# The low part of each weight tile formed by ScalarE's negated copy and an adding DMA, in place of VectorE's subtraction

## Chip, cores and metric

One core of one Trainium2 chip runs the kernel. The metric is the device time of one launch in microseconds (us). TensorE (PE) multiplies matrices, VectorE (DVE), ScalarE (ACT) and GpSimd (POOL) work on tiles in on-chip memory, and transfers are issued from the queues of SyncE (SP), ScalarE and GpSimd and carried by 16 DMA engines.

## What is computed

One layer of a decoder trunk for 512 prompt tokens and 8 sample tokens, model width 1024, everything in float32:

```python
x = x + W_out( sig(g_A) * (A(rmsnorm(x)) @ W_pA) + sig(g_B) * (B(rmsnorm(x)) @ W_pB) )
x = x + W_down( relu(rmsnorm(x) @ W_up)^2 )
# A: chunked gMLP spatial gating; B: 4 heads of chunkwise retention with a 256x512 state per head
# outputs: rmsnorm(x) of prompt and samples, new states of prompt and of the 8 samples, the gMLP's v rows
```

## The kernel before

Activations lie feature-major, 128 features by two halves of 260 tokens. The weights are the stationary operand. A float32 product is made of three passes over parts of lower precision: a weight tile is split into `wh`, the tile rounded to float32r, and `wl`, what the rounding left off, and the activations likewise (`xh`, `xl`). `prod` (L184) then issues wh*xh, wh*xl and wl*xh for both token halves: six matmuls for each 128-row slice of the weights.

All weights stream through one list of blocks, 88 of 1 MB, in the order of use (`build_stream`, L125). SP loads a block into one of three `raw` buffers (`load_to`, L147). A block is cut into four halves of 128x4x128 numbers (512 numbers on each partition, in four runs of 128). The generator `split` (L160) turns one half into a pair of tiles: L166 writes `wh` on ScalarE, L168 writes `wl` on VectorE, and the pair is entered in `wt`. There are five buffers each of `wh` and `wl` (`LA + 1`). `take` (L176) hands half i to the matmuls and before that starts the split of half i + 4. So the `wh` of half i + 4 takes the buffer that half i - 1 has just given up. A half is 24 matmuls. The first four halves are split apart from this, in `first_split` (L283); the other 348 go through `split`.

Work beside the stream is written as generators; `micro` (L76) moves each of them on by a step between matmuls, and a bare `yield` is one such step. This sets the order of the instructions on each engine by hand; every engine and queue works its instructions off in that order. The program's stages by the profile's time: the gMLP branch (to about 235 us), four retention heads (about 235 to 685), the joining of the branches and `w_out` (to about 765), the FFN (to about 1122), and the last norm.

Three places outside the stream matter. In the heads `samples` (L793) loads 64 slices of state on the SP queue (`sp_load`, L787), scales each on ScalarE (L821), updates it on VectorE (L823), stores it from the GpSimd queue (L824) and sums from it (L829), with four `sp` buffers. The GpSimd queue also carries the other stores to HBM and short power operations of the norms (L313, L707, L1043). A `raw` buffer is loaded anew (L158) when the last reader of the block that it held is done.

Of the kernel before, what the change touches and what calls it, by code (L numbers as in the profile page):

```python
# [11 lines left out]
AF = mybir.ActivationFunctionType  # L12
ALU = mybir.AluOpType
# [20 lines left out]
def f32(ap):  # L34
    return ap.bitcast(F32)
# [5 lines left out]

@with_exitstack
def trunk_kernel(ctx: ExitStack, tc: tile.TileContext, t: dict, o: dict):
    """Activations lie feature-major, [128 features, 2 halves, 256 prompt + 4 sample tokens]; the weights are the
    stationary operand. A float32 product runs as three float32r passes over exact parts (hi rounded to
    float32r, lo = x - hi): hi*hi + hi*lo + lo*hi. Work beside the weight stream is written as generators
    that advance between the matrix products."""
    nc = tc.nc
    V, S, PE, G = nc.vector, nc.scalar, nc.tensor, nc.gpsimd
    gam = [1.0 - 2.0 ** (-5.0 - h) for h in range(NH)]  # L50
# [10 lines left out]

    w_in = t["w_in"][0]

# [1 line left out]
    tasks, done = [], set()  # L65

    def advance(T):
# [30 lines left out]
            n += 1  # L98
            assert n < 2000, [k for k in keys if k not in done]

# [1 line left out]
    blocks, halves = [], []  # L102

    def add_block(src, uses):
# [55 lines left out]
    def split(i):  # L160
        b, k0, c0, _ = halves[i]
        load_to(b + (2 if i and halves[i - 1][0] == b else 1))
        src = raw_t[b][:, k0:k0 + 4, c0:c0 + 128]
        wh = st["wpool"].tile([P, 4, 128], R, tag="wh", bufs=st["wbufs"], name="wh")
        wl = st["wpool"].tile([P, 4, 128], R, tag="wl", bufs=st["wbufs"], name="wl")
        S.activation(out=wh, in_=src, func=AF.Copy)  # L166
        yield
        V.tensor_tensor(out=wl, in0=src, in1=f32(wh), op=ALU.subtract)  # L168
        wt[i] = (wh, wl)

    def split_to(n):
# [45 lines left out]
        return r[:, :512].rearrange("p (a b) -> p a b", a=4)  # L217

    def hilo(oh, ol, src):
        """Two steps: the rounded part, then the rest."""  # L220
        S.activation(out=oh, in_=src, func=AF.Copy)
        yield
        V.tensor_tensor(out=ol, in0=src, in1=f32(oh), op=ALU.subtract)
# [7 lines left out]
    def halves_of(pt):  # L231
        return pt.rearrange("p (h a) b -> p h (a b)", h=2)

# [1 line left out]
    gm = ExitStack()  # L235
    xp = ExitStack()
    xpool = xp.enter_context(tc.tile_pool(name="xpool", bufs=1, side="right"))
# [33 lines left out]
    for i in range(N_WARM):  # L271
        PE.matmul(ps_w[:, i % 2, :256], lhsT=warm[:, :P], rhs=warm, start=True, stop=True)

# [1 line left out]
    xh = xpool.tile([P, 8, 2, HC], R, name="xh")  # L275
    xl = xpool.tile([P, 8, 2, HC], R, name="xl")
    X = (xh, xl)
# [35 lines left out]
        G.tensor_tensor(out=dst, in0=dst, in1=neghalf[:n, :dst.shape[-1]], op=ALU.pow)  # L313

    def bcast_rows(rs, out, lag):
        """rs: [128, 5] per token (4 chunks, then the samples); out: [128, 2, 260], along the partitions."""
        dg = base.tile([P, 2 * HC], F32, tag="m4", bufs=2, name="dg")
        for c in range(4):
            V.tensor_scalar(out=dg[:, 128 * c:128 * (c + 1)], in0=ident, scalar1=rs[:, c:c + 1], scalar2=None,
                            op0=ALU.mult)  # L320
        V.tensor_scalar(out=dg[:NS, 512:520], in0=ident[:NS, :NS], scalar1=rs[:NS, 4:5], scalar2=None, op0=ALU.mult)
        yield lag
        pa = x_tile()
        pb = x_tile()
        PE.matmul(pa.rearrange("p a b -> p (a b)"), lhsT=ones, rhs=dg[:, :512], start=True, stop=True)
        PE.matmul(pb[:, 0, :8], lhsT=ones[:NS, :], rhs=dg[:NS, 512:520], start=True, stop=True)
        yield 2
        V.tensor_copy(out=out[:, :, 0:256], in_=halves_of(pa))
        V.tensor_copy(out=out[:, :, 256:HC], in_=hs8(pb[:, 0, :8]))
# [3 lines left out]
    rst = base.tile([P, 5], F32, name="rst")  # L333

    def token_rsqrt(pool, sq, key, lag):
        """rb = rsqrt(mean over the features + eps) from the sums of squares left on the partitions."""
        rs = rst
        sqs = pool.tile([P, 8], F32, name="sqs")
        V.memset(rs, 1.0)
        V.tensor_copy(out=hs8(sqs), in_=sq[:, :, 256:HC])  # L340
        yield lag[0]
        pt = x_tile()
        for c in range(4):
            hh, off = ccols(c)
            PE.matmul(pt[:, 0, c:c + 1], lhsT=sq[:, hh, off:off + 128], rhs=ones[:, 0:1], start=True, stop=True)
        PE.matmul(pt[:NS, 0, 4:5], lhsT=sqs, rhs=ones[:, 0:1], start=True, stop=True)
        yield
        V.tensor_copy(out=rs[:, 0:4], in_=pt[:, 0, 0:4])
        V.tensor_copy(out=rs[:NS, 4:5], in_=pt[:NS, 0, 4:5])
        rsqrt_mean(rs, rs, 1.0 / DM)  # L350
        yield lag[1]
        yield from bcast_rows(rs, rb, lag[2])
        done.add(key)
# [18 lines left out]
        V.tensor_tensor(out=z, in0=ps[:, :, :HC], in1=rb, op=ALU.mult)  # L372
        return z

# [1 line left out]
    smpv = gpool.tile([P, 8, 8], F32, name="smpv")  # L376
    lng = gpool.tile([P, DM], F32, name="lng")
    lnb = gpool.tile([P, DM], F32, name="lnb")
# [192 lines left out]
        micro()  # L571
    gm.close()

# [1 line left out]
    late = ctx.enter_context(tc.tile_pool(name="late", bufs=1))  # L575
    acc = late.tile([P, 8, 2, HC], F32, tag="acc", name="pbacc")
    hs = ExitStack()
# [31 lines left out]
    def make_head(h):  # L609
        H = Head()  # L610
        g = gam[h]
# [66 lines left out]
            done.add(("s", h))  # L678

        def v_task(e, ps):  # L680
            """v stays unscaled; its tokens' factors go into k and the scores."""
            z = tmp()
            S.copy(out=z, in_=ps[:, :, :HC])
            V.tensor_tensor(out=hs8(H.smp[:, 4 + e, :]), in0=z[:, :, 256:HC], in1=rb[:, :, 256:HC], op=ALU.mult)
            done.add(("vs", h, e))
            yield 2
            yield has(("s", h))
            if e == 0:
                H.vh = hp.tile([P, 4, DV], R, tag="vkh", name="vh")
                H.vl = hp.tile([P, 4, DV], R, tag="vkl", name="vl")  # L690
            pt = x_tile()
            for c in range(4):
                hh, off = ccols(c)
                PE.transpose(pt[:, c, :], z[:, hh, off:off + 128], ident)  # L694
            yield
            es = slice(128 * e, 128 * (e + 1))
            yield from hilo(H.vh[:, :, es], H.vl[:, :, es], pt)
            done.add(("vt", h, e))
# [14 lines left out]
            done.add(("o", h, c))  # L713

        def steps():
            """o of each chunk, token-major, and the state's update."""
            yield has(("kt", h), ("s", h), *[("vt", h, e) for e in range(4)])
            yield 2
            st_ps = ps_s.tile([P, 2, DV], F32, tag="st", name="st_ps")
# [70 lines left out]
                nc.sync.dma_start(out=H.sp[i], in_=sview[:, :, i, :])  # L790

        def samples():
            """The state's step of the samples: partitions hold (sample, 16 blocks of 16 rows of the state)."""  # L793
            yield has(*([("rs", h - 1)] if h else []), *[("vs", h, e) for e in range(4)])
            yield 3
            for j in range(2):
# [114 lines left out]
    until(*[("gb", m) for m in range(8)])  # L911
    xp.close()

# [1 line left out]
    f0s = ExitStack()  # L915
    f0 = f0s.enter_context(tc.tile_pool(name="f0", bufs=1, side="right"))
    h2 = (f0.tile([P, 8, 2, HC], R, name="hh_t"), f0.tile([P, 8, 2, HC], R, name="hl_t"))
# [61 lines left out]

    spawn(ffn_norm(), now=False)  # L980

# [1 line left out]
    F = {}  # L983

    def up_task(fh, f, ps):
# [19 lines left out]
        F["rs"] = pool.tile([P, 2, 3], F32, name="rs3")  # L1005

    def fin_task(m, ps, hhs):
        """x2 = x1 + the FFN's output; the sums of its squares, the last d-tile's apart."""
        a, b = hhs[0], hhs[-1] + 1
        x = x1[:, m, a:b]  # L1010
        V.tensor_tensor(out=x, in0=x, in1=ps[:, a:b, :HC], op=ALU.add)
        yield 1 if m == 7 else 1
        z = F["sq"][:, a:b] if m == 0 else F["z"][:, a:b] if m == 7 else tmp()[:, a:b]
        S.activation(out=z, in_=x, func=AF.Square)
        if 0 < m < 7:
            yield
            V.tensor_tensor(out=F["sq"][:, a:b], in0=F["sq"][:, a:b], in1=z, op=ALU.add)
        done.update(("fin", m, hh) for hh in hhs)
# [1 line left out]
    cols = (slice(0, 128), slice(128, 256), slice(HC - 128, HC))  # L1020

    def fin_norm(hh):
        """Token sums over the features, the samples' in the last rows of the third column."""
        yield has(*[("fin", m, hh) for m in range(7)])
        yield 17
        if hh:
# [77 lines left out]


def constants():
    """Tables that depend on shapes and positions alone."""
    a = np.arange(DK // 2, dtype=np.float32) * (np.float32(1) / np.float32(DK // 2 - 1))
    a[-1] = 1.0
    inv = np.float32(1) / (10000.0 ** a.astype(np.float64)).astype(np.float32)  # L1110
    pos = np.full((2, HC), PAST, np.float32)
    pos[0, :256] = np.arange(256)
    pos[1, :256] = np.arange(256, 512)
    ang = (inv[:, None, None] * pos[None]).astype(np.float32).astype(np.float64)
    j = np.arange(P, dtype=np.float64)
    tab = np.zeros((P, 544), np.float64)
    for h in range(NH):
        g = 1.0 - 2.0 ** (-5.0 - h)
        tab[:, 128 * h:128 * (h + 1)] = np.where(j[None, :] >= j[:, None], g ** -j[:, None], 0.0) / 16.0
        for c in range(4):  # L1120
            tab[:, 512 + 4 * h + c] = g ** -(128.0 * c + j) / 16.0
        tab[:, 528 + h] = g ** j
        tab[:, 532 + h] = g ** (2 * j) / DV
    for s in range(NS):
        tab[16 * s:16 * (s + 1), 536 + s] = 1.0
    return {"c_ident": np.eye(P, dtype=np.float32), "c_tab": tab.astype(np.float32),
            "c_cos": np.cos(ang).astype(np.float32), "c_sin": np.sin(ang).astype(np.float32)}
# [44 lines left out]
```

## Time and profile before

| | |
|---|---|
| time, median of two runs | 1148.82 us (1146.76 to 1150.87) |
| span of the profiled execution | 1145.0 us |
| granted TensorE clock over it | 0.995 of full speed |
| TensorE busy | 1125.9 us, 98% |
| VectorE / ScalarE / GpSimd busy | 670.1 / 476.3 / 89.2 us |
| moved by DMA | 148.05 MB |

The span runs from the first to the last instruction of one profiled execution; the runs' times contain a little more around it. Busy time of an engine leaves out the issuing of DMAs on SP and ScalarE, while GpSimd's own issues are counted. A DMA share is the mean share of time in which the 16 DMA engines worked on packets. An idle engine costs nothing by itself; what counts is whether the matmuls have to wait.

### The profile page before, as it was taken

Reading aid. Unit: us, or ns where it says so; the run is one execution under the profiler, and the core shown is the slowest. Engines: PE = TensorE matmul, PEld = TensorE weight load, DVE = VectorE, ACT = ScalarE, POOL = GpSimd, SP = SyncE. Lnnn points to the kernel's source line nnn. Section 1 sums busy time; section 2 is a strip of 40 time slices with the busy share of each in tenths; the row PEclk is TensorE's granted clock in tenths of the full one; section 3 lists DMA queues with packets and bytes.
Section 4 is the critical chain, followed back from the end, with each engine's and each line's share of the span. In section 5 each row is a group of like instructions: output and inputs, shape, how many; then the busy total and the mean of one; then the engine's idle time right before and its main releaser. Section 6 shows DMA issues by size and latency. Waiting matters only on the chain.

```text
span 1145.0 us, 21897 instructions
## 1 busy us (share of the span) xinstructions
PE 1125.9 (98%) x9134; PEld 1107.8 (97%) x9134; DVE 670.1 (59%) x1178; ACT 476.3 (42%) x844; POOL 89.2 (8%) x148
## 2 busy tenths in 40 slices
PE   8999999999999989999999999999999999999996
PEld 8999999999999989999999999999999999999996
DVE  6567833554984488477846878555553234554333
ACT  6465522246555545554555543432332222333220
POOL 0000000002110210120102120000000000000000
PEclk9999999999999999999999999999999999999998
DMA  8423233224673475356634795623232323232302
GB/s 290 130 82 103 76 112 129 94 74 141 183 205 126 117 218 177 100 146 194 172 120 117 206 316 160 194 77 109 74 110 76 111 74 109 77 106 80 100 12 75
DMA packets 116628, 148.05 MB, mean 129 GB/s; under 512 B 9576, under 2 KB 93736, under 8 KB 116528
## 3 DMA queue, kind: packets, MB, share of 16 engines
q1 hardware_dynamic: 101712, 118.73, 32.8%
q0 software_dynamic: 12336, 24.72, 7.8%
q10 hardware_dynamic: 2480, 3.19, 0.8%
q8 instruction: 72, 1.18, 0.5%
q14 instruction: 28, 0.23, 0.1%
HBM read 121.16 MB, written 25.43 MB: 128 GB/s over the span
## 4 chain that ended last, share of the span: by engine, by line
PE 83%; issue 8%; DMA 3%; DVE 2%; POOL 2%; ACT 1%; SPq 0%; ACTq 0%; POOLq 0%; DVEq 0%
PE mm L189 75%; PE xps L730 2%; PE st_ps L736 2%; DMA sp<-in_state_ret 2%; POOL out_new_s L824 1%; PE xps L694 1%; DMA xT<-in_xT 1%; PE ps_v L189 1%; DMA out_new_s<-sp 0%; DVE sp L823 0%; DVE wl L168 0%; PE xps L799 0%; ACT sp L821 0%; DVE so L829 0%; DVE x L1058 0%
## 5 line engine op out<-in xcount | busy, mean ns | idle before, releaser
L166 ACT ACTIVATE wh<-raw 128x512 fp32r<-128x512 f32 x348 | 218.9, 632 | 462.0 <-PE mm L189 442.9
L168 DVE TENSOR_TENSOR wl<-raw,wh 128x512 fp32r<-128x512 f32 x348 | 238.6, 688 | 201.3 <-ACT wh L166 199.7
L189 PE MATMUL mm<-xh,wh 128*128 128x260 f32 x1264 | 261.0, 288 | 2.2 <-ACT wh L287 0.8
L189 PE MATMUL mm<-xl,wh 128*128 128x260 f32 x1264 | 254.7, 283 | 0.3 <-DVE xl L294 0.3
L189 PE MATMUL mm<-xh,wl 128*128 128x260 f32 x1264 | 254.8, 283 | 0.0
L189 PEld LDWEIGHTS mm<-xh,wh 128*128 128x128 f32 x1264 | 196.2, 189 | 5.7 <-ACT wh L287 1.1
L189 PEld LDWEIGHTS mm<-xl,wh 128*128 128x128 f32 x1264 | 195.1, 189 | 0.8 <-DVE xl L294 0.8
L189 PEld LDWEIGHTS mm<-xh,wl 128*128 128x128 f32 x1264 | 195.4, 189 | 0.0
L189 PE MATMUL mm<-ah,wh 128*128 128x260 f32 x640 | 134.3, 283 | 0.0
L189 PE MATMUL mm<-ah,wl 128*128 128x260 f32 x640 | 134.1, 283 | 0.0
L189 PE MATMUL mm<-al,wh 128*128 128x260 f32 x640 | 134.0, 283 | 0.0
L189 PE MATMUL mm<-gh,wl 128*128 128x260 f32 x512 | 103.2, 283 | 0.0
L189 PE MATMUL mm<-gh,wh 128*128 128x260 f32 x512 | 103.2, 283 | 0.0
L189 PE MATMUL mm<-gl,wh 128*128 128x260 f32 x512 | 103.0, 283 | 0.0
L189 PEld LDWEIGHTS mm<-ah,wh 128*128 128x128 f32 x640 | 100.9, 188 | 0.0
L189 PEld LDWEIGHTS mm<-ah,wl 128*128 128x128 f32 x640 | 100.9, 188 | 0.0
L189 PEld LDWEIGHTS mm<-al,wh 128*128 128x128 f32 x640 | 100.6, 188 | 0.0
L372 DVE TENSOR_TENSOR tmp<-mm,rb 128x520 f32<-128x520 f32 x69 | 48.2, 698 | 72.0 <-PE mm L189 71.9
L189 PEld LDWEIGHTS mm<-gh,wh 128*128 128x128 f32 x512 | 78.9, 188 | 0.0
L189 PEld LDWEIGHTS mm<-gh,wl 128*128 128x128 f32 x512 | 79.0, 188 | 0.0
L189 PEld LDWEIGHTS mm<-gl,wh 128*128 128x128 f32 x512 | 78.7, 188 | 0.0
L824 POOL DMA_DIRECT2D out_new_s<-sp x64 | 39.2, 612 | 218.0 <-DVE sp L823 205.4
(280 smaller groups left out, 1467.1 us busy)
## 6 DMA issues: line engine op xcount, KB each, us to landing
raw<-in_w_in SPq DMA_DIRECT2D x39, 1024.0 KB
sp<-in_state_ret SPq DMA_DIRECT2D x64, 256.0 KB
out_new_s<-sp POOLq DMA_DIRECT2D x64, 256.0 KB, 5.0
raw<-in_w_up SPq DMA_DIRECT2D x16, 1024.0 KB
raw<-in_w_down SPq DMA_DIRECT2D x16, 1024.0 KB
raw<-in_w_proj_ret SPq DMA_DIRECT2D x8, 1024.0 KB
raw<-in_w_proj_gm SPq DMA_DIRECT2D x4, 1024.0 KB
raw<-in_w_out SPq DMA_DIRECT2D x4, 1024.0 KB
```

The source lines that it names most:

```text
L166: S.activation(out=wh, in_=src, func=AF.Copy)
L168: V.tensor_tensor(out=wl, in0=src, in1=f32(wh), op=ALU.subtract)
L189: PE.matmul(ps[:, hh, :HC], lhsT=w[:, j, :], rhs=x[:, k, hh, :], start=(first and q == 0), stop=(last and q == 2))
L372: V.tensor_tensor(out=z, in0=ps[:, :, :HC], in1=rb, op=ALU.mult)
L694: PE.transpose(pt[:, c, :], z[:, hh, off:off + 128], ident)
L730: PE.matmul(po, lhsT=a, rhs=b, start=(n == 0), stop=(n == len(mms) - 1))
L736: PE.matmul(st_ps[:, d, :], lhsT=a[:, c, ks], rhs=b[:, c, :], start=(c == 0 and n == 0), stop=(c == 3 and n == 2), skip_group_check=True)
L824: G.dma_start(out=oview[:, :, i, :], in_=sp)
```

## The change

After the rounding to `wh`, ScalarE writes `wl` too: a copy of `wh` times -1. One step of the generators later a DMA is issued from the GpSimd queue that adds the raw half onto it, so that `wl` = -wh + raw. VectorE's subtraction goes. `take` may hand the pair out at the same point of the program as before, since the DMA stands where the subtraction stood. `first_split` is as it was.

```diff
         S.activation(out=wh, in_=src, func=AF.Copy)
-        yield
-        V.tensor_tensor(out=wl, in0=src, in1=f32(wh), op=ALU.subtract)
+        S.activation(out=wl, in_=f32(wh), func=AF.Copy, scale=-1.0)
+        yield
+        G.dma_start(out=wl, in_=src, accum_op=ALU.add)
         wt[i] = (wh, wl)
```

Besides, comments and docstrings are blanked out, which leaves the instructions alone; behind L168 all lines move down by one.

## Rows read from the trace of the kernel before

**Rows 1.** The page: span, engines' busy time and share, the chain by engine.
```profile
span 1145.0 us, 21897 instructions
...
PE 1125.9 (98%) x9134; PEld 1107.8 (97%) x9134; DVE 670.1 (59%) x1178; ACT 476.3 (42%) x844; POOL 89.2 (8%) x148
...
PE 83%; issue 8%; DMA 3%; DVE 2%; POOL 2%; ACT 1%; SPq 0%; ACTq 0%; POOLq 0%; DVEq 0%
```
**Rows 2.** Timeline of ScalarE in the FFN: start, duration, instruction, idle before.
```profile
880.91 0.63 ACT L166 ACTIVATE wh<-raw 128x512 fp32r<-128x512 f32 x1 [2.23 <-PE mm L189]
883.81 0.63 ACT L166 ACTIVATE wh<-raw 128x512 fp32r<-128x512 f32 x1 [2.27 <-PE mm L189]
```
**Rows 3.** Stretches: length, busy of PE, PEld, DVE, ACT, POOL, clock, DMA share, GB/s.
```profile
2.00:28.00 26.00, 24.24 (x189) 22.67 (x188) 17.95 (x33) 17.79 (x33) 0.00 (x0) 1.00 0.94 318
...
235.00:685.00 450.00, 443.31 (x3486) 430.32 (x3485) 307.16 (x562) 236.12 (x443) 71.88 (x117) 1.00 0.55 162
```
**Rows 4.** Stretches, VectorE's `wl` alone: length, busy (count), clock, DMA share, GB/s.
```profile
28.00:140.00 112.00, 22.59 (x33) 1.00 0.30 95
140.00:235.00 95.00, 22.36 (x33) 1.00 0.35 118
235.00:300.00 65.00, 11.39 (x17) 1.00 0.38 111
300.00:340.00 40.00, 8.28 (x12) 1.00 0.74 207
340.00:390.00 50.00, 8.28 (x12) 1.00 0.38 120
390.00:430.00 40.00, 7.48 (x11) 1.00 0.70 199
430.00:560.00 130.00, 26.14 (x38) 0.99 0.53 154
560.00:685.00 125.00, 24.73 (x36) 1.00 0.62 187
685.00:765.00 80.00, 19.16 (x28) 1.00 0.52 163
765.00:1122.00 357.00, 83.66 (x122) 1.00 0.26 83
```
**Rows 5.** The chain that ended last, in order of time: start, length, what.
```profile
38.33 0.69 DVE wl L168
...
395.97 5.29 DMA sp<-in_state_ret
...
409.22 8.32 DMA sp<-in_state_ret
```
**Rows 6.** Waits: who waited for whom, us in total, times, longest.
```profile
POOL out_new_s L824 <- DVE sp L823: 205.4, 58, 8.1
...
SPq L158 <- DVE wl L168: 694.0, 65, 18.3
SPq L790 <- DMA out_new_s<-sp: 193.7, 47, 11.0
```
**Rows 7.** The page's costliest groups: the two halves of the split.
```profile
L166 ACT ACTIVATE wh<-raw 128x512 fp32r<-128x512 f32 x348 | 218.9, 632 | 462.0 <-PE mm L189 442.9
L168 DVE TENSOR_TENSOR wl<-raw,wh 128x512 fp32r<-128x512 f32 x348 | 238.6, 688 | 201.3 <-ACT wh L166 199.7
```
**Rows 8.** The state's stores at L824: durations (ns) on GpSimd, and to landing.
```profile
L824 POOL DMA_DIRECT2D out_new_s<-sp x64: 596/598/872, 279.8 to 673.9; - x64
...
DMA to landing us min/median/max: 3.9/5.0/8.5
```
**Rows 9.** DMA queues from 815 to 950 us, SP's: packets, MB, share of 16 engines.
```profile
q1 hardware_dynamic: 12346, 12.46, 28.7%
```
**Rows 10.** DMA queues from 235 to 685 us, GpSimd's own.
```profile
q0 software_dynamic: 11264, 21.23, 17.8%
```

## Prediction

> **What bounds the kernel now.** I read the page first: TensorE is busy for 98% of a span of 1145.0 us, and the chain that ended last runs through it for 83% [rows 1]. VectorE (59%) and ScalarE (42%) are far from full. All that TensorE leaves idle is 1145.0 - 1125.9 = 19.1 us, 1.7%, start and end included, so relief for another engine can't be worth more than that; in the heads it is 450 - 443.31 = 6.7 us [rows 3].
>
> Next the timeline, to see how much room a weight half has. In the FFN ScalarE begins a `wh` every 2.9 us, idle before each for 2.2 us until TensorE gives a buffer up [rows 2]. A half of 24 matmuls thus takes 2.9 us, and this is the period of the stream. By the code the `wh` that begins when half i - 1 ends belongs to half i + 4, so four halves lie between, 4 x 2.9 = 11.6 us. Today's split takes 0.63 + 0.69 us of that: about 10 us of slack.
>
> Then the stretches, for the DMA engines. Their share is 0.55 over the heads [rows 3], but 0.26 in the FFN and 0.62 to 0.74 in three parts of the heads [rows 4]. There the state's loads lie on the chain, 5.3 and 8.3 us long [rows 5], and SP waits 193.7 us for state stores to land before it can load again [rows 6]. So in the FFN only TensorE is short; in the heads TensorE and DMA are both near their limits.
>
> **The change, part by part.**
>
> *Removed:* 348 subtractions of 688 ns, 239 us of VectorE [rows 7]. They are hidden behind matmuls except where VectorE runs late; the gain lies between nothing and the 6.7 us of gaps in the heads. I take nothing, since the same places also wait for state loads.
>
> *Added on ScalarE:* 348 copies of the shape of L166, so 348 x 0.632 = 220 us [rows 7]; ScalarE goes from 476 to 696 us, 61%. In the FFN the second copy fits into the 2.2 us idle before each `wh` [rows 2]; over the heads 236 us becomes 236 + 126 x 0.63 = 315 us of 450 [rows 3, 4]. I cost it at nothing; were the cover gone it would be 0.63 us for each half that TensorE waits for.
>
> *Added latency:* `wl` is ready when the DMA has landed. The nearest rows are stores of the same 256 KB from the same queue: 3.9 us to landing at least, 5.0 median, 8.5 at most [rows 8]. With two copies (1.3 us) that makes 6.3, typically, and 9.8 at worst, under 11.6. In the steady stages nothing is lost. At the start the chain runs through a `wl` at 38.33 us [rows 5], where 0.69 us is replaced by about 5: +5 us, rounded up for the first halves.
>
> *Added on the GpSimd queue:* 348 issues between stores and power operations. A DMA of 128 runs takes 0.60 us there [rows 8]; an adding one has 512 runs of 512 bytes. From below it takes 0.6 us, if runs cost nothing; from above 4 x 0.6 x 3/2 = 3.6 us, if time goes with runs and two reads and a write count for three instead of two. I take about 1.2, nearer to the lower end, because an issue's time has a part that doesn't depend on runs; then 348 x 1.2 = 418 us lies beside the matmuls. An add waits on its queue for ScalarE, which waits for TensorE, up to 2.3 us [rows 2]; queued behind it are the state's stores, and for them SP's next state load. The other way round an add stands behind a store that waits up to 8.1 us for VectorE [rows 6]. VectorE's subtraction stood behind the same instruction, so only the DMA's own latency is new.
>
> *Moved on SP's queue:* a `raw` buffer is free when the last add has landed, some 5 us later than now. SP's wait at L158 (694 us in 65 [rows 6]) grows by that. A block is next used nine halves, 26 us, later, so the weights come in time; state loads queued behind it are late by up to 5 us.
>
> *Added on the DMA engines,* which decides. An add has 128 x 4 = 512 runs, 32 for each of the 16 engines. In the FFN the weight loads' packets, 1 KB each, take 0.287 x 16 x 135 us / 12346 = 50 ns [rows 9]. A run is 512 bytes read from raw, 512 read from `wl`, and 512 written. If the two reads go one after the other, it costs a 1 KB packet: 32 x 50 ns = 1.6 us an add. From below, half a packet, as a plain copy of 512 bytes might cost: 0.8 us. From above, one packet of the GpSimd queue in the heads, 0.178 x 16 x 450 / 11264 = 114 ns [rows 10]: 3.6 us. I take 1.6, since the bytes read are those of the first row, and that row too goes into on-chip memory, while the last one is mostly stores to HBM.
>
> *The sum.* Work of the DMA engines in a stretch is share x length, plus 1.61 us for each add, one for each subtraction of today [rows 4]. Back-to-back loads at the start reach a share of 0.94 [rows 3], so a stretch can't be shorter than work / 0.94. This gives:
> 300 to 340: (29.6 + 19.3) / 0.94 = 52.0, +12.0;
> 390 to 430: (28.0 + 17.7) / 0.94 = 48.6, +8.6;
> 430 to 560: (68.9 + 61.2) / 0.94 = 138.4, +8.4;
> 560 to 685: (77.5 + 58.0) / 0.94 = 144.1, +19.1;
> 685 to 765: (41.6 + 45.1) / 0.94 = 92.2, +12.2.
> In the FFN (92.8 + 196.4) / 0.94 = 308 stays under 357 us, +0; the other four stretches stay under too (28 to 140 us, the fullest: (33.6 + 53.1) / 0.94 = 92 of 112). Together +60, with the start +65: 1145 + 65 = 1210 us of span. The median of the runs is 3.8 us above the profiled span, so 1214 us.
>
> **The rivals.** *Hidden (the other side: not slower).* The DMA engines take an add in 0.8 us, as a copy. Then only 300 to 340 is over its length, (29.6 + 9.6) / 0.94 = 41.7, +1.7, and with the start's 5 the time is 1156 us; with the 6.7 us of gaps won back, 1149. It decides below about 1.1 us an add, where the loss falls under 2%. For it: the slack of 10 us covers the latency. Against it: an add has to read its target as well.
> The Trainium skill, "DMA: Bandwidth & Descriptors", section on the anatomy of one DMA on the GpSimd path, fits 2.0 us plus bytes / 436 GB/s to one DMA; by that an estimate for 256 KB is 2.6 us, of which 0.6 us is movement, and this rival would hold at about 1150 us. The trace shows 3.9 to 8.5 us to landing for stores of that size [rows 8], longer than the rule.
> Another page, "Collectives: The Full Stack", section "The bandwidth ceiling", speaks against this rival: an add in a DMA needs two source reads on one ring and so moves at half a copy's rate. No row of the kernel before shows an add.
>
> *The add is dearer than the stream's period.* If DMA engines or GpSimd need more than a half's 2.9 us, less the weight loads, every stage waits, the FFN too; it decides from (357 x 0.94 - 92.8) / 122 = 2.0 us an add on the DMA engines. At the middle between my value and the upper bound, 2.6 us, the same sum gives +82 in the FFN, +165 in the heads, +42 in the stage behind them and +48 before them: about 1490 us. If it is GpSimd at 3.6 us, 348 x 3.6 + 89 = 1342 us. For it: 512 short runs in place of 128 on a queue that a program feeds, and nothing in the trace that adds. Against it: the issue rows are flat at 0.60 us.
>
> *Faster.* All 6.7 us in the heads and some of the rest come back: 1138 us at best by the traced gaps, under 1%. More than 2% is beyond the 19.1 us that there are.
>
> **How the numbers follow.** DMA engines full in the heads and behind them, 1172 to 1290 us: 0.40, the likeliest, 1214 us. Hidden: 0.31, of which 0.01 faster. Dearer than the period: 0.29. The range leaves out the upper part of the dear case (0.12) and a small part of the hidden one: 1142 to 1490 us. About 2%, 23 us, is what a measurement of this kernel tells from no change. Slower by more: 0.40 + 0.29 = 0.69, less 0.01 for the lower edge of the likeliest case, 0.68; within 2%: 0.31; faster: 0.01.
>
> **What would show it.** VectorE's L168 is gone (about 430 us busy), ScalarE is near 696 us. The GpSimd group for `wl` has 348 issues: a mean of 0.9 to 1.5 us is right, over 2.9 wrong. The DMA share in the FFN should be (92.8 + 196) / 357 = 0.81 with the same 2.9 us period; a share of 0.55 speaks for the hidden case, 0.94 with a longer period for the dear one. In the heads it should be near 0.94 with TensorE idle for tens of us, its waits on the add. What would make the prediction wrong at once: an add that costs far from 50 ns a run, in either direction.

## The result and the profile after

The changed kernel takes 1259.32 us (1256.15 to 1262.49) beside 1148.82 us: a ratio of 1.097, 95% interval 1.088 to 1.106. That is 110 us more; +65 was forecast.

The page of the changed kernel, its header, engines, slices and the queue that GpSimd issues to:
```profile
span 1254.4 us, 22599 instructions
...
PE 1160.1 (92%) x9134; PEld 1132.0 (90%) x9134; DVE 461.8 (37%) x830; ACT 687.9 (55%) x1192; POOL 534.2 (43%) x496
...
DMA  9999999987998889979999999999999999999993
...
q0 software_dynamic: 196080, 115.97, 69.2%
...
PE 62%; DMA 17%; issue 8%; POOL 6%; ACT 3%; DVE 2%; SPq 0%; POOLq 0%; DVEq 0%; ACTq 0%
...
L169 POOL DMA_DIRECT2D wl<-raw x348 | 449.8, 1301 | 505.2 <-ACT wl L167 423.2
L167 ACT ACTIVATE wl<-wh 128x512 fp32r<-128x512 f32 x348 | 220.0, 632 | 11.1
```
The subtractions are gone and ScalarE has its 348 copies. The DMA engines are busy in nearly every slice. In the chain DMA has gone from 3% to 17% [rows 1].

Where the time went can be read by counting the stream's matmuls, which are the same 8448 in the same order in both traces. The matmul that starts at the times on the left in the trace of before starts so much later in that of after:

| before, us | stage that ends there | later by, us | of it in this stage |
|---|---|---|---|
| 28 | first halves | 8.3 | +8.3 |
| 235 | gMLP | 8.7 | +0.4 |
| 685 | four heads | 102.7 | +94.0 |
| 765 | joining, w_out | 108.1 | +5.4 |
| 1110 | FFN but its last 12 us | 108.1 | 0.0 |
| 1122 | end of the FFN | 109.9 | +1.8 |

Stretches of the changed kernel (length, busy of PE, PEld, DVE, ACT, POOL, clock, DMA share, GB/s): a part of the gMLP, the heads, and most of the FFN:
```profile
140.00:235.00 95.00, 95.00 (x792) 94.80 (x792) 23.55 (x42) 48.93 (x80) 45.28 (x40) 1.00 1.10 196
...
244.00:788.00 544.00, 473.02 (x3487) 451.10 (x3485) 235.12 (x436) 310.55 (x568) 235.34 (x242) 0.94 0.96 195
...
880.00:1200.00 320.00, 320.00 (x2666) 320.00 (x2665) 75.07 (x112) 158.63 (x257) 140.22 (x111) 1.00 1.07 181
```
Beside [rows 3], the heads take 544 us in place of 450 for the same matmuls (3486 and 3487), with TensorE idle for 71 us in place of 6.7. The busy time of these matmuls grew too, from 443.3 to 473.0 us, at a granted clock of 0.94. In these parts of the gMLP and the FFN TensorE doesn't lose a microsecond, at DMA shares of 1.10 and 1.07: the times of packets then overlap on an engine, and add up to more than the stretch. A full share by itself costs nothing, then. What the heads have besides are the state's loads and stores, for which other engines wait.

The adds themselves: first a DMA query from 900 to 1100 us (packets, MB, share; the add's issues, KB each, us to landing), then the issues from 243 to 788 us:
```profile
q0 software_dynamic: 36366, 18.06, 78.5%
...
wl<-raw POOLq DMA_DIRECT2D x69, 256.0 KB, 5.3
...
wl<-raw POOLq DMA_DIRECT2D x126, 256.0 KB, 9.3
...
out_new_s<-sp POOLq DMA_DIRECT2D x64, 256.0 KB, 8.8
...
row_d<-srow POOLq DMA_DIRECT2D x8, 16.0 KB, 6.2
```
One run of 512 bytes takes 0.785 x 16 x 200 / 36366 = 69 ns of an engine, an add 32 x 69 = 2.2 us. It lands 5.3 us after its issue in the FFN and 9.3 us after it in the heads. There the other stores of the GpSimd queue land later too, the state's 8.8 us after their issue in place of 5.0 [rows 8].

### The profile page after: what moved, and what is told of

Read it like the earlier page. It is cut to its first block, busy times and chain, and to the rows that moved or that the text cites. A ratio compares the mean times of both kernels' runs of the same rounds, so it can differ in the third digit from the quotient of the medians.

```text
span 1254.4 us, 22599 instructions
## 1 busy us (share of the span) xinstructions
PE 1160.1 (92%) x9134; PEld 1132.0 (90%) x9134; DVE 461.8 (37%) x830; ACT 687.9 (55%) x1192; POOL 534.2 (43%) x496
## 4 chain that ended last, share of the span: by engine, by line
PE 62%; DMA 17%; issue 8%; POOL 6%; ACT 3%; DVE 2%; SPq 0%; POOLq 0%; DVEq 0%; ACTq 0%
PE mm L190 57%; DMA wl<-raw 8%; DMA sp<-in_state_ret 4%; POOL wl L169 3%; DMA row_d<-srow 3%; POOL out_new_s L825 1%; DMA out_new_s<-sp 1%; PE st_ps L737 1%; PE xps L731 1%; DMA raw<-in_w_in 1%; ACT wh L166 1%; DMA ld<-gb_d 1%; ACT wl L167 1%; ACT sp L822 1%; PE xps L695 1%
## 5 line engine op out<-in xcount | busy, mean ns | idle before, releaser
L169 POOL DMA_DIRECT2D wl<-raw x348 | 449.8, 1301 | 505.2 <-ACT wl L167 423.2
L190 PE MATMUL mm<-xh,wl 128*128 128x260 f32 x1264 | 263.3, 291 | 38.6 <-DMA wl<-raw 38.4
L190 PE MATMUL mm<-xh,wh 128*128 128x260 f32 x1264 | 267.6, 294 | 8.2 <-ACT pbacc L871 4.1
L190 PEld LDWEIGHTS mm<-xh,wl 128*128 128x128 f32 x1264 | 201.0, 194 | 43.4 <-DMA wl<-raw 43.4
L167 ACT ACTIVATE wl<-wh 128x512 fp32r<-128x512 f32 x348 | 220.0, 632 | 11.1
L190 PEld LDWEIGHTS mm<-xh,wh 128*128 128x128 f32 x1264 | 202.9, 195 | 12.0 <-ACT pbacc L871 4.3
L190 PEld LDWEIGHTS mm<-xl,wh 128*128 128x128 f32 x1264 | 200.8, 194 | 0.6 <-DVE xl L295 0.5
L825 POOL DMA_DIRECT2D out_new_s<-sp x64 | 47.7, 754 | 103.3 <-DVE sp L824 95.8
L824 DVE SCALAR_TENSOR_TENSOR sp<-vp,kp,sp 128x512 f32<-128x512 f32 x64 | 48.0, 750 | 104.9 <-ACT sp L822 104.8
L822 ACT ACTIVATE sp<-sp 128x512 f32<-128x512 f32 x64 | 39.7, 621 | 83.2 <-DMA sp<-in_state_ret 71.2
```

The lines of the kernel that those rows point to most:

```text
L167: S.activation(out=wl, in_=f32(wh), func=AF.Copy, scale=-1.0)
L169: G.dma_start(out=wl, in_=src, accum_op=ALU.add)
L190: PE.matmul(ps[:, hh, :HC], lhsT=w[:, j, :], rhs=x[:, k, hh, :], start=(first and q == 0), stop=(last and q == 2))
L822: S.mul(out=sp, in_=sp, mul=float(g))
L824: V.scalar_tensor_tensor(out=sp, in0=vp, scalar=kp[:, i:i + 1], in1=sp, op0=ALU.mult, op1=ALU.add)
L825: G.dma_start(out=oview[:, :, i, :], in_=sp)
```

## Experiments

The theories. **A**: TensorE waits for adds that land late. **B**: GpSimd's queue, in which adds, stores and power operations stand behind each other. **C**: whoever reads the adds, they take the DMA engines from the heads' other transfers, the state's loads and stores above all. **D**: ScalarE's extra copies. Each run was timed beside the kernel before, which took 1146.8 to 1147.8 us in the three groups.

**D alone.** ScalarE's copy stays, VectorE adds, no DMA:
```diff
-        G.dma_start(out=wl, in_=src, accum_op=ALU.add)
+        V.tensor_tensor(out=wl, in0=src, in1=f32(wl), op=ALU.add)
```


> ScalarE writes the sign-turned copy as in the change, but VectorE does the adding (same count and shape as its subtraction before); no DMA is added. Theory A (the loss of 110 us is TensorE waiting for adds that land late where state traffic and adds share the DMA engines) and B (GpSimd's queue in order) expect the time of before, 1149 us, within 6. Theory D (the 220 us of extra copies on ScalarE, in order ahead of other work) expects a good part of the loss, over 1180 us.


Measured: 1157.4 us, ratio 1.009 (1.007 to 1.011). By the matmul count 2.3 us of it fall at the start, 2.1 in the gMLP, 5.9 in the heads. D is not the cause, but the copies, with VectorE's wait for them, are not free: about 10 us, more than the 6 that A and B allowed.

**Adds in the heads alone.**
```diff
...
-        S.activation(out=wl, in_=f32(wh), func=AF.Copy, scale=-1.0)
-        yield
-        G.dma_start(out=wl, in_=src, accum_op=ALU.add)
+        if in_heads(i):
+            S.activation(out=wl, in_=f32(wh), func=AF.Copy, scale=-1.0)
+            yield
+            G.dma_start(out=wl, in_=src, accum_op=ALU.add)
+        else:
+            yield
+            V.tensor_tensor(out=wl, in0=src, in1=f32(wh), op=ALU.subtract)
```


> Adding DMAs for the weights used in the retention heads alone (136 of 348 halves); all others by VectorE's subtraction as before. The two traces put 94 us of the loss into the heads, 8 at the start, 5 behind the heads, 0 in the gMLP and the FFN. If that split is right and the stages don't help each other, 1149 + 94 + at most 5 = 1243 to 1250 us. If the DMA work in the FFN also costs (share over 1.0 there) it would be below 1235.


Measured: 1250.1 us, ratio 1.090 (1.087 to 1.093), the sum that the stages gave. The trace counts 144 such adds (the 136 of the expectation leave out the last head's projection); they cost 103 us. What remains of the changed kernel's loss, some 7 us, goes with the 204 others and their copies, at the start.

**Adds that nobody reads.** The kernel before with, behind VectorE's subtraction:
```diff
         V.tensor_tensor(out=wl, in0=src, in1=f32(wh), op=ALU.subtract)
+        G.dma_start(out=src.bitcast(R), in_=f32(wh), accum_op=ALU.add)
```


> The kernel before, and beside it for each half an adding DMA of the same 512 runs of 512 bytes on GpSimd's queue (wh added onto the half of raw that has been read for the last time), which no product reads. The buffers of wh and raw still wait for it to land. Theory A: TensorE doesn't wait for adds, so most of the loss goes, 1150 to 1185 us. Theory C (adds slow the state's loads and stores and through them ScalarE, VectorE and TensorE, whoever reads the add): most of the loss stays, 1220 to 1270. Theory B (order on GpSimd's queue): stores stand behind adds here too, over 1200.


Measured: 1254.4 us, ratio 1.092 (1.089 to 1.095), the time of the changed kernel. Here no matmul waits for an add, VectorE has its old load and ScalarE no copies; only the buffers that an add reads or writes wait for it to land. The heads of this run as a stretch:
```profile
239.00:789.00 550.00, 472.06 (x3485) 452.46 (x3484) 306.24 (x562) 234.37 (x443) 235.47 (x243) 0.92 0.94 191
```
And its longest waits in the heads (us in total, times, longest):
```profile
ACT sp L822 <- DMA sp<-in_state_ret: 109.5, 24, 12.6
POOL out_new_s L825 <- DVE sp L824: 103.2, 28, 12.0
...
DVE ss L710 <- POOL ss L708: 40.7, 9, 9.7
```
The same two waits in the heads of the kernel before:
```profile
ACT sp L821 <- DMA sp<-in_state_ret: 26.4, 12, 3.8
...
DVE ss L709 <- POOL ss L707: 10.6, 8, 2.9
```
A falls: the changed kernel has TensorE wait about 40 us for adds, but with that wait taken away as much time goes to others. ScalarE waits 109.5 us for state loads, where it waited 26.4 us before and 71.2 us in the changed kernel. VectorE waits 40.7 us for power operations on GpSimd, 10.6 us before and 41.5 us in the changed kernel.

**The same issues, few bytes.** As before, with 8 bytes a run:
```diff
+        G.dma_start(out=src[:, :, :2].bitcast(R), in_=f32(wh[:, :, :2]), accum_op=ALU.add)
```


> As the run before it, but each of the 512 runs of an add has 8 bytes in place of 512: GpSimd issues as many descriptors, while the DMA engines move 1/64 of the bytes. Theory B (GpSimd's issue time and order) expects the same time as with the full runs. Theories A and C (the DMA engines' time) expect about the time of before, up to 1165 us. If runs cost the DMA engines a fixed time and bytes nothing, both are the same too, which the packets' times tell apart.


Measured: 1173.6 us, ratio 1.023 (1.021 to 1.026): 27 us over the kernel before, more than C allowed for, far less than B. GpSimd is as busy (534.1 us), so the other 81 us of the run with full adds come of the bytes alone. The 27 us are not GpSimd's alone, since a run of 8 bytes isn't free on the DMA engines. GpSimd's DMA queue over the whole program (packets, MB, share) in the kernel before, with 8-byte runs, with half the bytes (the next experiment), and with the full adds that nobody reads:
```profile
q0 software_dynamic: 12336, 24.72, 7.8%
...
q0 software_dynamic: 196080, 26.17, 34.1%
...
q0 software_dynamic: 106992, 70.36, 39.8%
...
q0 software_dynamic: 196080, 115.97, 68.8%
```
Times the spans, and less the 89 us of the kernel before, an add of 8-byte runs takes (399 - 89) / 348 = 0.9 us of the DMA engines, an add with half the bytes 1.1 us, a full one 2.2 us. How the 27 us divide between these 0.9 us and GpSimd's queue is not shown. Order on that queue has a part in them: VectorE's wait for power operations is 29.6 us here (10.6 before).

**Half the bytes.** Two of the four runs of each partition by DMA, two by VectorE:
```diff
-        S.activation(out=wl, in_=f32(wh), func=AF.Copy, scale=-1.0)
+        S.activation(out=wl[:, 2:], in_=f32(wh[:, 2:]), func=AF.Copy, scale=-1.0)
         yield
-        G.dma_start(out=wl, in_=src, accum_op=ALU.add)
+        V.tensor_tensor(out=wl[:, :2], in0=src[:, :2], in1=f32(wh[:, :2]), op=ALU.subtract)
+        G.dma_start(out=wl[:, 2:], in_=src[:, 2:], accum_op=ALU.add)
```


> Half of each wl by the adding DMA (256 runs of 512 bytes), the other half by VectorE's subtraction; as many issues on GpSimd as in the change. Theory C with a loss in proportion to bytes: 1174 + 40 = 1205 to 1220 us. Theory C with a threshold (the DMA engines have room up to about 1 us an add): under 1190. Theory B: near the changed kernel, over 1235.


Measured: 1181.5 us, ratio 1.029 (1.026 to 1.031). The first half of the bytes costs 34 us, the second half 78, for 1.1 us an add each: the loss grows faster than the work. That it is only 8 us more than with 8-byte runs says little, since the two differ by 0.2 us an add (and the 8-byte run has no copies on ScalarE). The heads as a stretch:
```profile
242.00:720.00 478.00, 452.81 (x3479) 436.21 (x3477) 277.31 (x561) 284.90 (x567) 224.35 (x242) 0.98 0.79 186
```

**Without the state's stores.** The 64 stores at L825 of the changed kernel are left out, so the samples' new states are never written:
```diff
-                G.dma_start(out=oview[:, :, i, :], in_=sp)
```


> The changed kernel without the 64 stores of the new sample states (the output new_s is left out: 16.8 MB of writes, and a state buffer is free again as soon as it has been summed). Theory C, in which a load waits for a store that lands late beside the adds: the heads lose at most 30 us, 1155 to 1190 us. If it is TensorE's waits on the adds themselves, or clock and matmuls, that hold the heads, most of the loss stays: over 1220.


Measured: 1209.2 us, ratio 1.052 (1.049 to 1.055), between the two expectations: 49 us come back of the 110, and 61 stay. The heads:
```profile
245.00:739.00 494.00, 459.39 (x3481) 440.83 (x3480) 235.07 (x436) 310.87 (x568) 190.07 (x178) 0.96 0.92 179
```
So the stores are a good part of what the adds collide with, but not all of it. The edit takes away more than bytes: GpSimd waits 95.8 us in the heads of the changed kernel for VectorE before these stores, with adds behind them, and SP 171.7 us for them to land. Which of the three gives the 49 us is not shown, and the kernel before was not run without its stores; TensorE idles for only 6.7 us in its heads.

**The stores on SP's queue,** in the changed kernel and, as a control, in the one before:
```diff
-                G.dma_start(out=oview[:, :, i, :], in_=sp)
+                nc.sync.dma_start(out=oview[:, :, i, :], in_=sp)
```


> The changed kernel with the 64 state stores issued from SP's queue, so that no store stands behind an add on GpSimd's queue. The run with 8-byte runs put 27 us on GpSimd's issues and order, the bytes on the DMA engines 80 us more. Theory B (order on GpSimd's queue): the 27 us go, 1230 us or less. Theory C (adds take the DMA engines from the state's loads and stores): 1245 to 1265 us.

> The control: the kernel before with the 64 state stores on SP's queue. SP then waits for VectorE's update before it goes on to weight loads that have 20 us to spare. Both theories expect 1147 us within 10; what it differs from before is taken off the run with the change.


Measured: 1291.3 us (1.124, 1.121 to 1.127) and 1158.9 us (1.009, 1.007 to 1.011). The control is 11 us slower, just outside what was expected, and the changed kernel loses 33 us more than it did; neither theory had that. SP's queue now waits for VectorE, with the loads behind it (waits of SP, us in total, times, longest, of the changed kernel with this edit):
```profile
SPq L825 <- DVE sp L824: 48.5, 13, 17.7
SPq L825 <- DVE Sl L748: 47.9, 3, 23.9
SPq L825 <- DVE so L828: 26.2, 1, 26.2
```
The experiment traded one in-order queue for a worse one, and says little of B.

**The sample rows off GpSimd's queue.** The trace of after shows one hold-up on that queue in full (GpSimd from 274 to 291 us: start, length, instruction, idle before):
```profile
274.33 1.08 POOL L809 DMA_DIRECT2D row_d<-srow  x1
279.56 0.68 POOL L814 DMA_DIRECT2D qp<-row_d  x1 [4.16 <-DMA row_d<-srow]
280.23 0.62 POOL L815 DMA_DIRECT2D kp<-row_d  x1
284.95 0.58 POOL L816 DMA_DIRECT2D vp<-row_d  x1 [4.11 <-DMA row_d<-srow]
285.55 0.58 POOL L708 TENSOR_TENSOR ss<-ss,neghalf 128x1 f32<-128x1 f32 x1
286.08 1.39 POOL L169 DMA_DIRECT2D wl<-raw  x1
```
The row loads wait for two 16 KB stores to land, and a power operation of 0.6 us stands behind them. VectorE waits for that one, and TensorE for VectorE (waits from 281 to 288 us):
```profile
DVE ss L710 <- POOL ss L708: 10.5, 1, 10.5
...
PE xps L731 <- DVE Sl L748: 5.5, 1, 5.5
```
The edit, in the changed kernel:
```diff
-                G.dma_start(out=row_d[h][:, 512 * j:512 * (j + 1)], in_=srow)
+                nc.scalar.dma_start(out=row_d[h][:, 512 * j:512 * (j + 1)], in_=srow)
...
-            G.dma_start(out=qp, ...)   # kp, vp likewise
+            nc.sync.dma_start(out=qp, ...)
```


> The changed kernel with the sample rows' 8 stores (row_d) issued from ScalarE's queue and their 12 loads (qp, kp, vp) from SP's. In the trace of the changed kernel GpSimd stands for about 11 us at the first head (274.9 to 285.0 us) for the row stores to land, with an add and a power operation behind it, and TensorE behind these. If such stands cost what they last, four heads x 7 to 10 us come back: 1217 to 1235 us. If the time is only shifted to the next wait on the DMA engines: 1245 us or more.


Measured: 1240.2 us, ratio 1.081 (1.077 to 1.085), between the two expectations again: about 18 us come back. In the heads of this run VectorE waits 8.8 us for power operations in place of 41.5, so order on GpSimd's queue does cost time. By the matmul count the run is 22 us ahead of the changed kernel at 560 us of before's time (51.6 us behind before in place of 74.0), but only 11.6 ahead at 685 us (91.1 in place of 102.7); the traced execution is the slowest of its four. The edit also puts a new hold-up on another queue: SP waits 38.6 us in the heads for the row stores to land, with state loads behind. The 18 us are what is left of both.

**Less room for the add, more for the state.** A lookahead of three halves; then besides six state buffers in place of four; then both in the kernel before:
```diff
-LA = 4
+LA = 3
...
-                H.sp[i] = hp.tile([P, DV], F32, tag="sp", bufs=4, name="sp")
+                H.sp[i] = hp.tile([P, DV], F32, tag="sp", bufs=6, name="sp")
...
-            for i in range(3):
+            for i in range(5):
                 sp_load(i)
...
-                sp_load(i + 3)
+                sp_load(i + 5)
...
```


> The changed kernel with a lookahead of three halves in place of four (buffers of wh and wl from five to four), so 8.7 us of room for a half in place of 11.6. In the FFN copies and add take 1.3 + 5.3 us, so it should lose nothing there. In the heads an add lands 9.3 us after its issue (median): if TensorE's wait on adds is a main cost there, 1290 us or more; if the state's chain sets the pace and adds only wait beside it, as the run whose adds nobody reads suggests, 1255 to 1285.

> As the run before it, and the 4 KB a partition that this frees go to two more state buffers (six in place of four, loads issued two slices earlier). Theory C (a state load waits for a store that lands late, and ScalarE and VectorE stand in order behind the load): 25 to 50 us less than the run before it. If the state's round trip is not what holds the heads: within 10 us of it.

> The kernel before with the same two settings (lookahead three, six state buffers). Its split needs 1.3 us of 8.7, so the shorter lookahead should cost at most 10 us; the longer state ring can win back part of the 6.7 us that TensorE is idle in the heads: 1137 to 1158 us.


Measured: 1259.6 us (1.098, 1.093 to 1.103), 1253.5 us (1.092, 1.085 to 1.098) and 1137.6 us (0.991, 0.989 to 0.993). With a quarter less room TensorE's waits on adds grow (whole run, us in total, times, longest, at a lookahead of three):
```profile
PE mm L190 <- DMA wl<-raw: 63.6, 36, 6.6
```
That is 24 us more than in the changed kernel (39.6). 13 of them lie in the heads (51.1 in place of 38.4 us), and yet by the matmul count the heads lose 81 us to the kernel before in place of 94: there a wait on an add only displaces others. From 685 us on the run loses 18.6 us in place of 7.2, 8.0 of them in the FFN in place of 1.8. So in the FFN 8.7 us of room is too little where 11.6 was enough but for the end, and the whole time stays because a gain and a loss cancel. Two more state buffers give 6 us, inside the intervals, so nothing shows the state's ring of buffers to hold the heads of the changed kernel; C in that narrow form falls too. In the kernel before the same edit gives 9.7 us, and that version beats both kernels: its heads take 441 us with TensorE busy for 440.6.

**What is left standing** is C in its wide form: the DMA engines' work. Length of the heads against DMA share x length, from the stretches of each run:

| kernel | heads, us | DMA share | work, us |
|---|---|---|---|
| before | 450 | 0.55 | 248 |
| adds of 8-byte runs | 475 | 0.75 | 356 |
| half the bytes | 478 | 0.79 | 378 |
| no state stores | 494 | 0.92 | 454 |
| rows off GpSimd | 531 | 0.98 | 520 |
| adds nobody reads | 550 | 0.94 | 517 |
| changed kernel | 544 | 0.96 | 522 |
| stores on SP's queue | 575 | 0.90 | 518 |

Up to a share of 0.8, 130 us of added work lengthen the heads by 28 us; the next 144 us lengthen them by 66. The table orders the runs and proves no limit: the gMLP and the FFN pass at 1.10 and 1.07 without a loss, and the last row has the work of the changed kernel and 31 us more. What the runs show is that taking bytes off the DMA engines gave most back: 81 us where nothing else was changed, 78 us with half of the adding on VectorE again, 49 us with the stores and their waits gone. Removing one wait at a time (reading the adds, room for them, state buffers, row loads) gave 0 to 18.

Not separated: SP's queue. Weight loads there wait for adds to land (in the heads 237 us in all with 8-byte runs, 295 us with full adds that nobody reads), and state loads stand behind them. How much of the 81 us comes by this way, and how much by transfers that take longer once they are issued, is open.

## Why the prediction was right, point by point

*The bound and the direction.* Right. The adds' work on the DMA engines costs its time in the heads and hardly any in the FFN, and nothing is won elsewhere: VectorE's 208 us less (670.1 to 461.8) shows in no stage; the run that keeps the subtraction and has the same adds is not slower, though it is also spared ScalarE's copies. The sign named for the heads came out in its numbers (a share of 0.96, TensorE idle for 71 us), but of the idle time only 38.4 us are waits on the add, and the run whose adds nobody reads has the loss without them.

*The size of an add* is the term that was too small: 1.61 us from a 1 KB packet at 50 ns [rows 9], 2.2 us measured, since a run of 512 bytes takes 69 ns and not 50. The Trainium skill, "Collectives: The Full Stack", section "The bandwidth ceiling", has an add in a DMA at half a copy's rate for its two reads. The direction agrees, but two reads of 512 bytes at the rate of [rows 9] would be 50 ns, and the trace has 69. By the other rule, of the Trainium skill, "DMA: Bandwidth & Descriptors", section on the anatomy of one DMA, an estimate for these 256 KB is 2.6 us. The trace has 5.3 us to landing in the FFN and 9.3 in the heads, and the measurement decides.

*The heads*: +48 forecast (12.0 + 8.6 + 8.4 + 19.1), +94 measured. With 2.2 us an add the same sum over the same four stretches gives (29.6 + 26.4) / 0.94 = 59.6, +19.6; (28.0 + 24.2) / 0.94 = 55.5, +15.5; (68.9 + 83.6) / 0.94 = 162.2, +32.2; (77.5 + 79.2) / 0.94 = 166.7, +41.7: together +109, and +1.1 more from 235 to 300 us. So a dearer add would fill the gap, and more than all of it, but the sum doesn't say where: by the matmul count 16.1 of the 94 us fall from 235 to 300 and from 340 to 390 us, where even at 2.2 us it has +1.1. GpSimd's order (within the 27 us of the 8-byte runs) and ScalarE's copies (6 us in the heads) are in the 94 as well.

*The ceiling of 0.94 and the threshold of 2.0 us* failed. By my sum a dearer add, at 2.2 us, had to stall the FFN: (92.8 + 122 x 2.2) / 0.94 = 384 us for 357. It lost 1.8 us at its end, at a share of 1.07. The gMLP from 140 to 235 us, fuller in the sum than the stretch that I called the fullest (92 of its 95 us at 1.6 us an add), had to stall from 1.7 us an add on; it lost 0.2 us, at 1.10. A mean share of 0.94 is thus no ceiling, since the times of packets overlap, and adds with 10 us of slack are indifferent to their own lateness. The same error made the stage behind the heads +12 in place of +5.4. Two errors of opposite sign, then, and the likeliest case came out right by its place, low by its size; that they partly cancel is luck. Another slip: by the same sum the loss passes 2% at 1.24 us an add, not at 1.1.

*Latency.* Right for the FFN: copies 1.3 and landing 5.3 us under 11.6. In the heads the median of 9.3 with 1.3 leaves under 1 us; the slack was spent there, but the run whose adds nobody reads and the heads at a lookahead of three show no cost of its own.

*The start*: 5 us forecast, 8.3 measured, of which the copies alone make 2.3 (the run for D). The first add lands late beside the loads that fill the DMA engines (chain of the changed kernel: start, length, what):
```profile
18.12 8.34 DMA wl<-raw
```

*GpSimd's issue*: 1.2 us estimated, 1.30 measured, 450 us in all. That it costs nothing but issue time was wrong: VectorE's waits for the power operations grew from 10.6 to 41.5 us, and taking the row loads off that queue gave 18 us back. I had argued that VectorE's subtraction stood behind the same instructions; what stands behind the adds now, the power operations for which VectorE waits, was not named.

*ScalarE*: costed at nothing, 10 us measured. In the FFN, where ScalarE idles before each `wh`, the copies cost nothing by the matmul count; the loss lies at the start, in the gMLP and in the heads.

*The clock* was not in the sum at all. Three stretches of the changed kernel, while TensorE has work, idles, and goes on:
```profile
275.00:281.00 6.00, 6.00 (x46) 5.66 (x45) 0.65 (x2) 3.98 (x6) 1.69 (x3) 1.00 0.82 200
281.00:288.00 7.00, 1.51 (x5) 0.74 (x4) 1.17 (x4) 0.92 (x2) 2.51 (x3) 0.83 0.39 109
288.00:294.00 6.00, 6.00 (x26) 5.22 (x27) 0.92 (x3) 3.21 (x7) 1.88 (x2) 0.63 0.77 90
```
After 5.5 us without work the granted clock is 0.63 of full speed (a mix of the levels 2.4 and 1.2 GHz). Two matmuls of the stream after the idle time, and two after the clock had risen to the upper level:
```profile
289.18 0.64 PE L190 MATMUL mm<-xh,wh 128*128 128x260 f32 x2
...
292.77 0.41 PE L190 MATMUL mm<-xh,wh 128*128 128x260 f32 x2
```
The heads' matmuls took 473.0 - 443.3 = 29.7 us more busy time, at a mean clock of 0.94, a good quarter of the whole loss. It is a consequence of the waits, and comes on top of them.

## What to carry to other kernels

Work moved off an engine that isn't the bound bought nothing here, and a DMA that does arithmetic isn't free work: price its runs, and look at the stage in which other engines wait for transfers, not at the mean share. When several in-order queues wait for the same busy engines, taking away one wait moves much of the time to the next; less work on the shared resource gave most back. An add that nobody reads, issued beside the old code, tells contention from dependence in one run.

## What the runs showed of the hardware that was not expected

- A DMA that adds 512-byte runs on chip takes 69 ns a run of an engine's time (a plain 1 KB packet: 50 ns), and GpSimd 1.30 us to issue 512 of them, 1.22 us to issue 256 (0.60 us for a store of 128 runs).
- An added run of 8 bytes still takes 0.9 us / 32 = 28 ns of an engine.
- The DMA share stood at 1.07 over 320 us of the FFN with TensorE busy throughout.
- An idle time of 5.5 us on TensorE was followed by a granted clock of 0.63 over the next 6 us.
- The power operation of 128 numbers on GpSimd took 0.56 us before; VectorE waited up to 10.5 us for it when adds and row loads stood ahead of it.
